# A bank of its own for p5 in the inner Strassen level of a float32 encoder block

## The chip, the core and the metric

The kernel runs on one core of one Trainium2 chip. The metric is the time of one execution on the device, in microseconds (us). The median of three runs of the kernel before is given below, and beside it one further execution that was recorded by the hardware profiler. Engines are named as in the profile: PE multiplies matrices, PEld loads its weights, ACT and DVE do elementwise work, SP issues transfers. A "bank" is a PSUM buffer of 128 partitions x 512 float32 numbers, into which PE adds its products.

## The reference

The reference is one layer of an encoder on 1024 tokens of width 1024, in float32: a SwiGLU pair around a token mixer, all with RMS norms and residual sums.

```python
h = x + 0.5 * swiglu_ffn(rmsnorm(x), ffn1_w_in, ffn1_w_out)      # hidden width 2816
proj = rmsnorm(h) @ w_in                                         # 1024 -> 7168: q k v g p and two gates
ret = retention(rotary(q), rotary(k) / 16, v)                    # 4 heads of 256, chunks of 64
ret = rmsnorm_per_head(ret) * silu(g)
pool_out = multiscale_pool(p, pool_w, pool_scale)
merged = sigmoid(gate_0 + b0) * (ret @ w_ret_up) + sigmoid(gate_1 + b1) * (pool_out @ w_pool_up)
h = h + merged @ w_out
h = h + 0.5 * swiglu_ffn(rmsnorm(h), ffn2_w_in, ffn2_w_out)
return rmsnorm(h)
```

Nearly all of the work is in the matrix products with the weights.

## The kernel before

**Products.** Activations lie with features on the 128 partitions and tokens along the row. Each float32 operand is split into a coarse part and a remainder (ACT casts, L151; DVE subtracts, L152), and one product of two such operands is three matmuls: coarse by coarse (L171), coarse by remainder (L172), remainder by coarse (L173), written together as `mm3`.

**The outer Strassen level.** The input products of both SwiGLU pairs and the combined projection are done by `strassen` (L391). One call, a group, makes two 128-row output tiles of 1024 tokens. It forms seven block products, each of 4 x 3 matmuls on 512 tokens, in place of eight. The banks of a group are `a`, `e` (from a pool of six, tag "ps") and the sum bank `b` (from a pool of two, tag "sum"). P3, the product of the weight combination S4 with the activation block R22, is the one on which the inner level works.

**The inner level.** `pairs` (L550) runs the groups two by two, first all steps of group A, then all of group B. For the pairs that share (`shared`), it leaves P3 out of both and runs `third` (L491) after them, which does P3 of A and B together with a second level of Strassen's scheme: seven products of half the width, 2 x 3 matmuls on 256 tokens each, so 42 matmuls. There are 8 such pairs in the first SwiGLU, 10 in the projection and 8 in the second SwiGLU, 26 in all; in this text each such call is "a third".

**Order within a third.** By the source, one third is these steps. `LO` and `HI` are the left and the right 256 columns of a 512-wide tile.

- p1: weights `wx`, six matmuls into the bank `x`, left half (L519). ACT copies that half to A's buffer `z` (L521).
- p5: weights `ws12` with the activation combination `y1`, six matmuls into the right half of the same bank `x` (L522). The first of them has no start flag. ACT copies this half to B's `z` (L524).
- p2: weights `wx`, six matmuls onto A's sum bank `b`, left half (L525).
- p6 (named so here): weights `ws12` with `y2`, six matmuls added to p1 in the left half of `x` (L529). DVE adds the copied p5 to it and writes A's `z`, right half (L531).
- Six matmuls with `ws34` onto A's `b`, right half (L532). Then DVE takes A's result out of `b` and `z` (L534, seen in the trace as line 631 or 990).
- Six matmuls with `wy` onto B's `b`, left half (L538).
- p7 (named so here): weights `ws34` with `y3`, six matmuls added to the left half of `x` (L539). ACT copies it to B's `z`, left half (L541), DVE adds to B's `z`, right half (L542), and B's result is taken out.

The weights of a third are split by `prep1` to `prep3`, which run four steps ahead of their products (`LOOK`, L51).

**What sets the order on an engine.** The source is written for a framework that orders each engine's queue and adds the waits between engines. An instruction can stand earlier in its queue than in the source when those before it are expected not to be ready; `soon()` (L98) raises the priority of what is inside it. In the trace of before, four of the six matmuls of p2 stand ahead of p5 on PE for this reason. Banks of a pool are handed out by the framework, and a bank is free again when the last reader of its holder is done.

**Names in the profile.** Buffer numbers are left out, so the bank `x` of a third is `a_x` in the first SwiGLU, `c_x` in the second, and `q0x`, `k0x`, `p1x` ... in the projection. The buffers `z` of both groups are `a_z` (or `c_z`) alike in the SwiGLUs; in the projection A's and B's have different names, as `q0z` and `t1z`.

Of the kernel before, what the change touches and what calls it, by code (L numbers as in the profile page):

```python
# [89 lines left out]
def block_kernel(ctx: ExitStack, tc, x, x_tok, vecs, f1_in, f1_out, w_in, pool_w, w_ret, w_pool, w_o,  # L90
# [6 lines left out]
    copy = nc.scalar.copy  # L97
# [25 lines left out]
    def c2(name):  # L123
        return sb.tile([P, H], F32, tag="c2", bufs=N_C2, name=name)

    def bank(name):
        return ps.tile([P, H], F32, tag="ps", name=name)

    def sum_bank(name):

        return ps.tile([P, H], F32, tag="sum", bufs=N_SUM, name=name)
# [10 lines left out]
    LO, HI = slice(0, HD), slice(HD, H)  # L142
# [20 lines left out]
    def weights(src, name):  # L163
        w = wt(name)
        n = src.shape[-1] // P
        split(flat(w, 0, n), flat(w, 1, n), src)
        return w

    def mm3(dst, w, m, start, stop):

        mm(dst, w[0], m[0], start=start, stop=False, skip_group_check=True)  # L171
        mm(dst, w[0], m[1], start=False, stop=False, skip_group_check=True)  # L172
        mm(dst, w[1], m[0], start=False, stop=stop, skip_group_check=True)  # L173

    def parts(m, at=slice(None)):
        return m[:, 0, at], m[:, 1, at]
# [12 lines left out]
    for n in range(N_SUM):  # L189
        b = sum_bank(f"set{n}")  # L190
# [300 lines left out]
    def third(nx, A, B):  # L491

        w, t, a, b = {}, {}, A.t, B.t

        def prep1():
            w["x"] = weights(a["S4"], f"{A.name}wx")
            s = t["s"] = c2(f"{A.name}s12")
            tt(s[:, LO], b["S4"][:, LO], b["S4"][:, HI], ADD)
            tt(s[:, HI], s[:, LO], a["S4"][:, LO], SUB)
            w["s12"] = weights(s, f"{A.name}ws12")  # L500

        def prep2():
            s = c2(f"{A.name}s34")
            tt(s[:, LO], a["S4"][:, LO], b["S4"][:, LO], SUB)
            tt(s[:, HI], a["S4"][:, HI], t["s"][:, HI], SUB)
            w["s34"] = weights(s, f"{A.name}ws34")

        def prep3():
            w["y"] = weights(b["S4"][:, HI], f"{A.name}wy")

        def prod(dst, n, at, m, start=False):
            for z in range(2):
                mm3(dst, parts(w[n], at + z), nx.block(m, z), start and z == 0, z == 1)


        def one():
            x = t["x"] = bank(f"{A.name}x")
            a["z"], b["z"] = c2(f"{A.name}z"), c2(f"{B.name}z")
            prod(x[:, LO], "x", 0, (0, 0), True)  # L519
            with soon():  # L520
                copy(a["z"][:, LO], x[:, LO])  # L521
            prod(x[:, HI], "s12", 0, "y1")  # L522
            with soon():
                copy(b["z"][:, HI], x[:, HI])  # L524
            prod(a["b"][:, LO], "x", 2, (1, 0))  # L525

        def two():
            x = t["x"]
            prod(x[:, LO], "s12", 2, "y2")  # L529
            with soon():  # L530
                tt(a["z"][:, HI], x[:, LO], b["z"][:, HI], ADD)  # L531
            prod(a["b"][:, HI], "s34", 2, (1, 1))  # L532
            with soon():
                A.third()  # L534

        def three():
            x = t["x"]
            prod(b["b"][:, LO], "y", 0, "y4")  # L538
            prod(x[:, LO], "s34", 0, "y3")  # L539
            with soon():  # L540
                copy(b["z"][:, LO], x[:, LO])  # L541
                tt(b["z"][:, HI], x[:, LO], b["z"][:, HI], ADD)  # L542
                B.third()

        return [(prep1, one), (prep2, two), (prep3, three)]


# [1079 lines left out]
```

## Time and profile before

| | |
|---|---|
| median of three runs | 2189.65 us (2189.18 to 2190.84) |
| profiled execution, its own time | 2191.3 us |
| its span on the core | 2189.3 us |
| DVE busy | 1788.2 us (82%) |
| ACT busy | 1038.8 us (47%) |
| PE clock granted, mean | 0.999 |
| transfers | 311.96 MB, 142 GB/s on the mean |

The profiled execution's own time is 2.0 us above its span. Every figure of an instruction below is from this execution. In a timeline the first column is the start in us from the span's beginning, the second the duration; in brackets stands how long the engine had been idle before the instruction, and who ended that. Matmuls overlap: a duration of 0.28 us goes with a start every 0.12 us, so a gap on PE is read from starts and not from the busy time.

### The profile page before, as it was taken

The page shows a single profiled execution, that of the slowest core. Times are in us where ns is not written, and L with a number is a line of the kernel's source. Part 1 is how long each engine was busy: PE and PEld are TensorE (multiplying, and loading weights), DVE is VectorE, ACT ScalarE, POOL GpSimd, SP SyncE. Part 2 cuts the span into 40 slices and gives each one's busy share as a digit, 9 for nine tenths or more (in the row PEclk, how much of TensorE's full clock was granted, in tenths as well). Part 3 has the DMA queues.
Part 4 walks back from the last instruction along what each step waited for, and adds up shares of the span by engine and source line. Part 5 has one row for each costly group of instructions (what it writes and reads, how often), then busy time and mean ns, then how long its engine had stood idle before and what let it go on. Part 6 is the DMA issues. An engine that isn't in the chain of part 4 may idle for free.

```text
span 2189.3 us, 29019 instructions
## 1 busy us (share of the span) xinstructions
PE 2176.3 (99%) x10556; PEld 1828.1 (84%) x10556; DVE 1788.2 (82%) x3068; ACT 1038.8 (47%) x1911; POOL 0.2 (0%) x4
## 2 busy tenths in 40 slices
PE   9999999999999999999999999999999999999998
PEld 7888888888888888888888998878888888888888
DVE  8797878888787687888887787799987878788774
ACT  8443434445554434344446663456633434344461
POOL 0000000000000000000000000000000000000000
PEclk9999999999999999999999999999999999999999
DMA  6233322596323332323345557524232322359522
GB/s 232 85 125 106 126 92 98 177 338 212 104 92 116 112 131 94 126 96 116 116 163 192 184 187 272 191 87 143 79 135 82 125 92 89 128 180 336 181 82 78
DMA packets 110447, 311.96 MB, mean 142 GB/s; under 512 B 12384, under 2 KB 13536, under 8 KB 110304
## 3 DMA queue, kind: packets, MB, share of 16 engines
q1 hardware_dynamic: 110304, 310.11, 41.4%
q8 instruction: 83, 1.36, 0.3%
q14 instruction: 60, 0.49, 0.1%
HBM read 219.36 MB, written 90.70 MB: 142 GB/s over the span
## 4 chain that ended last, share of the span: by engine, by line
PE 95%; DVE 2%; ACT 1%; DMA 1%; issue 0%; SPq 0%; DVEq 0%; ACTq 0%
PE c_b L171 2%; PE c_b L173 2%; PE c_b L172 2%; PE a_b L173 2%; PE a_b L172 2%; PE a_b L171 2%; PE c_a L172 2%; PE c_a L171 2%; PE c_a L173 2%; PE c_e L171 2%; PE c_e L172 2%; PE a_a L172 2%; PE a_a L171 2%; PE a_a L173 2%; PE a_e L173 2%; PE c_e L173 2%
## 5 line engine op out<-in xcount | busy, mean ns | idle before, releaser
L151 ACT CAST c_wS<-c_S 128x512 fp32r<-128x512 f32 x72 | 44.8, 622 | 70.8 <-DVE c_S L405 40.8
L172 PE MATMUL c_a<-n3R,c_wL 128*128 128x512 f32 x176 | 68.7, 390 | 0.0
L173 PE MATMUL c_a<-n3R,c_wL 128*128 128x512 f32 x176 | 68.5, 389 | 0.0
L172 PE MATMUL c_b<-n3T,c_wS 128*128 128x512 f32 x176 | 68.5, 389 | 0.0
L173 PE MATMUL c_b<-n3T,c_wS 128*128 128x512 f32 x176 | 68.5, 389 | 0.0
L171 PE MATMUL c_a<-n3R,c_wL 128*128 128x512 f32 x176 | 68.4, 390 | 0.0
L171 PE MATMUL c_b<-n3T,c_wS 128*128 128x512 f32 x176 | 68.2, 389 | 0.0
L171 PE MATMUL a_a<-n1R,a_wL 128*128 128x512 f32 x168 | 65.5, 390 | 0.0
L172 PE MATMUL a_a<-n1R,a_wL 128*128 128x512 f32 x168 | 65.5, 390 | 0.0
L171 PE MATMUL a_b<-n1T,a_wS 128*128 128x512 f32 x168 | 65.4, 389 | 0.0
L173 PE MATMUL a_b<-n1T,a_wS 128*128 128x512 f32 x168 | 65.4, 389 | 0.0
L173 PE MATMUL a_a<-n1R,a_wL 128*128 128x512 f32 x168 | 65.4, 389 | 0.0
L172 PE MATMUL a_b<-n1T,a_wS 128*128 128x512 f32 x168 | 65.4, 389 | 0.0
L151 ACT CAST a_wS<-a_S 128x512 fp32r<-128x512 f32 x68 | 42.1, 620 | 48.0 <-DVE a_S L405 24.2
L152 DVE TENSOR_TENSOR a_wS<-a_S,a_wS 128x512 fp32r<-128x512 f32 x68 | 46.3, 683 | 5.0 <-ACT a_wS L151 4.8
L152 DVE TENSOR_TENSOR c_wS<-c_S,c_wS 128x512 fp32r<-128x512 f32 x72 | 49.2, 684 | 1.2 <-ACT c_wS L151 1.0
L151 ACT CAST c_wL<-c_ra 128x512 fp32r<-128x512 f32 x44 | 27.1, 619 | 29.3 <-PE c_e L173 22.4
L151 ACT CAST a_wL<-a_ra 128x512 fp32r<-128x512 f32 x42 | 26.0, 621 | 29.8 <-PE a_e L173 22.6
L173 PEld LDWEIGHTS c_a<-n3R,c_wL 128*128 128x128 f32 x176 | 33.0, 188 | 6.9
L172 PEld LDWEIGHTS c_a<-n3R,c_wL 128*128 128x128 f32 x176 | 33.1, 188 | 6.9 <-DVE n3R L156 0.3
L172 PEld LDWEIGHTS c_b<-n3T,c_wS 128*128 128x128 f32 x176 | 33.0, 188 | 6.9
L171 PEld LDWEIGHTS c_b<-n3T,c_wS 128*128 128x128 f32 x176 | 33.0, 188 | 6.9
(2947 smaller groups left out, 7718.0 us busy)
## 6 DMA issues: line engine op xcount, KB each, us to landing
c_ra<-in_f_in SPq DMA_DIRECT2D x22, 512.0 KB, 3.6
c_rb<-in_f_in SPq DMA_DIRECT2D x22, 512.0 KB, 4.0
a_ra<-in_f_in SPq DMA_DIRECT2D x21, 512.0 KB, 3.9
a_rb<-in_f_in SPq DMA_DIRECT2D x21, 512.0 KB, 4.6
t<-au SPq DMA_DIRECT2D x11, 512.0 KB, 2.6
b<-an SPq DMA_DIRECT2D x11, 512.0 KB, 2.8
r<-au SPq DMA_DIRECT2D x11, 512.0 KB, 3.0
bra<-in_f_out SPq DMA_DIRECT2D x11, 512.0 KB, 5.9
```

What stands on the lines that cost most here:

```text
L151: copy(hi, src)
L152: tt(lo, src, hi.bitcast(F32), SUB)
L171: mm(dst, w[0], m[0], start=start, stop=False, skip_group_check=True)
L172: mm(dst, w[0], m[1], start=False, stop=False, skip_group_check=True)
L173: mm(dst, w[1], m[0], start=False, stop=stop, skip_group_check=True)
```

## The change

Within a third, p5 no longer goes to the right half of the bank `x`. A second bank `y` is taken from the pool of six at the same place, p5 goes to the right half of `y`, with a start flag of its own on its first matmul, and ACT's copy to B's `z` reads it there. The left half of `x` is used as before, its right half and the left half of `y` are not used. A pair with a third takes six banks from that pool in place of five. Nothing else is edited; the number of matmuls, copies, additions and transfers is the same.

```diff
         def one():
-            x = t["x"] = bank(f"{A.name}x")
+            x, y = (bank(f"{A.name}{n}") for n in "xy")
+            t["x"] = x
             a["z"], b["z"] = c2(f"{A.name}z"), c2(f"{B.name}z")
             prod(x[:, LO], "x", 0, (0, 0), True)
             with soon():
                 copy(a["z"][:, LO], x[:, LO])
-            prod(x[:, HI], "s12", 0, "y1")
+            prod(y[:, HI], "s12", 0, "y1", True)
             with soon():
-                copy(b["z"][:, HI], x[:, HI])
+                copy(b["z"][:, HI], y[:, HI])
             prod(a["b"][:, LO], "x", 2, (1, 0))
```

## The prediction

> **What bounds the kernel.** I read the page first, then the list of waits, then the timeline of one third. The page says that PE sets the time.
>
> ```profile
> span 2189.3 us, 29019 instructions
> ...
> PE 2176.3 (99%) x10556; PEld 1828.1 (84%) x10556; DVE 1788.2 (82%) x3068; ACT 1038.8 (47%) x1911; POOL 0.2 (0%) x4
> ...
> PE 95%; DVE 2%; ACT 1%; DMA 1%; issue 0%; SPq 0%; DVEq 0%; ACTq 0%
> ```
>
> The second line is busy time, the third the share of each engine in the chain that ended last. PE is on that chain for 95% of the span, so a gap removed from PE's queue shortens the time by its length, unless something else becomes late there. Such gaps are few, and the list of waits of PE's weight loads (us in total, times, longest) names most of them:
>
> ```profile
> PEld wo1b L171 <- ACT wo1wS L151: 2.1, 1, 2.1
> PEld c_x L171 <- ACT c_z L524: 2.0, 8, 0.2
> PEld a_x L171 <- ACT a_z L524: 1.9, 8, 0.2
> PEld a_x L171 <- ACT a_z L521: 1.6, 8, 0.2
> PEld c_x L171 <- ACT c_z L521: 1.5, 8, 0.2
> PEld xb L171 <- ACT state L151: 1.4, 2, 0.8
> ...
> PEld k0x L171 <- ACT t2z L524: 0.2, 1, 0.2
> ...
> PEld q1x L171 <- ACT q1z L521: 0.2, 1, 0.2
> ```
>
> Each third has two waits of the same kind: a product into `x` waits for ACT's copy out of `x` (L521 for the left half, L524 for the right). They come eight times each in both SwiGLUs, and the ten thirds of the projection have a row of 0.2 us each for L524 and for L521, of which one each is shown. Nothing else on PE repeats like this.
>
> The timeline of the first third shows what they cost:
>
> ```profile
> 139.72 0.28 PE L171 MATMUL a_x<-n1R,a_wx 128*128 128x256 f32 x1
> ...
> 140.32 0.28 PE L173 MATMUL a_x<-n1R,a_wx 128*128 128x256 f32 x1
> ...
> 140.69 0.37 ACT L521 COPY a_z<-a_x 128x256 f32<-128x256 f32 x1
> ...
> 140.80 0.28 PE L171 MATMUL a_b<-n1R,a_wx 128*128 128x256 f32 x1
> ...
> 141.12 0.19 PEld L171 LDWEIGHTS a_x<-n1y,a_ws 128*128 128x128 f32 x1 [0.24 <-ACT a_z L521]
> ...
> 141.34 0.28 PE L172 MATMUL a_x<-n1y,a_ws 128*128 128x256 f32 x1
> ...
> 142.30 0.28 PE L172 MATMUL a_b<-n1R,a_ws 128*128 128x256 f32 x1
> ...
> 142.56 0.19 PEld L171 LDWEIGHTS a_x<-n1y,a_ws 128*128 128x128 f32 x1 [0.19 <-ACT a_z L524]
> ...
> 142.78 0.28 PE L172 MATMUL a_x<-n1y,a_ws 128*128 128x256 f32 x1
> ...
> 143.26 0.28 PE L173 MATMUL a_x<-n1y,a_ws 128*128 128x256 f32 x1
> ...
> 143.65 0.42 DVE L531 TENSOR_TENSOR a_z<-a_x,a_z 128x256 f32<-128x256 f32 x1 [0.53 <-PE a_x L173]
> ...
> 145.30 0.40 PE L171 MATMUL a_a<-n1R,a_wL 128*128 128x512 f32 x1
> ```
>
> The six matmuls of p1 start from 139.72 to 140.32, and four matmuls of p2 follow, the last at 140.80. That is 1.08 us for nine steps, 0.12 us a step. p5 writes the right half, which the copy doesn't read, and yet its first weight load waits until the copy ends (140.69 + 0.37 = 141.06) and starts 0.06 us later. What is kept apart is thus the bank and not the columns. p6 then waits in the same way for the copy of p5, although it writes the left half.
>
> **Cost of the two waits.** From the matmul before the gap to the second one behind it, two steps at 0.12 us would be 0.24 us. The first gap takes 141.34 - 140.80 = 0.54, a loss of 0.30 us; the second 142.78 - 142.30 = 0.48, a loss of 0.24 us. About 0.2 us of each is the wait, and the rest is that the first matmul behind it needs 0.22 us to the next start. Together 0.54 us. The check is the third as a whole: 145.30 - 139.72 = 5.58 us for 42 matmuls, which at 0.12 us are 5.04 us, and 0.54 us remain. The last of the 26 thirds gives the same:
>
> ```profile
> 1921.89 0.28 PE L171 MATMUL c_x<-n3R,c_wx 128*128 128x256 f32 x1
> ...
> 1922.97 0.28 PE L171 MATMUL c_b<-n3R,c_wx 128*128 128x256 f32 x1
> ...
> 1923.46 0.28 PE L172 MATMUL c_x<-n3y,c_ws 128*128 128x256 f32 x1
> ...
> 1924.41 0.28 PE L172 MATMUL c_b<-n3R,c_ws 128*128 128x256 f32 x1
> ...
> 1924.95 0.28 PE L172 MATMUL c_x<-n3y,c_ws 128*128 128x256 f32 x1
> ```
>
> Here it is 0.49 - 0.24 = 0.25 and 0.54 - 0.24 = 0.30, 0.55 us. I take 0.545 us for each third.
>
> The step of 0.12 us is the row's. [...]
>
> **What goes, part by part.** p5 gets bank `y`, so it shares no bank with p1's copy, and the first wait goes. p6 adds to `x`; the copy of p5 now reads `y`, so the second wait goes as well. What p6 needs from then on is the copy of p1 (L521) alone. With no wait PE can follow the source: p1, p5, p2, p6 and so on. p6 would start 18 steps after 139.72, at 139.72 + 18 x 0.12 = 141.88, while that copy ends at 141.06: 0.76 us to spare after the 0.06 us of signalling.
>
> p5 would start six steps in, at 140.44 instead of 141.12. Its weights have long been there (first row):
>
> ```profile
> 133.58 0.68 DVE L152 TENSOR_TENSOR a_ws<-a_s,a_ws 128x512 fp32r<-128x512 f32 x1
> ...
> 139.95 0.68 DVE L631 TENSOR_TENSOR au<-a_e,a_v 128x512 f32<-128x512 f32 x1
> ...
> 142.44 0.68 DVE L637 TENSOR_TENSOR au<-au,n1rb 128x512 f32<-128x512 f32 x1
> ```
>
> Nothing is added on any engine: the same 42 matmuls, two copies, and the start flag is a field of a matmul that is there anyway. I cost the flag at nothing: p1's first matmul carries one and takes the same 0.28 us. No transfer moves.
>
> What is late next is p7, which adds to `x` and must wait for DVE's L531. p6's last matmul would start at 139.72 + 23 x 0.12 = 142.48. In before L531 starts 143.65 - 143.26 = 0.39 us after that start, so it would be ready at 142.87; the addition in front of it on DVE starts at 142.44 and such instructions start 0.6 us apart (757.21 and 757.82 below), so L531 runs from 143.04 to 143.46. p7 would start 36 steps in, at 144.04. That leaves 0.52 us after the signal. One third is tighter, the first of the projection, where a 1024-wide instruction stands ahead:
>
> ```profile
> 753.87 0.28 PE L171 MATMUL q0x<-n2R,q0wx 128*128 128x256 f32 x1
> ...
> 755.98 1.22 DVE L970 TENSOR_TENSOR cos<-cos,n2rb 128x1024 f32<-128x1024 f32 x1
> ...
> 757.21 0.69 DVE L152 TENSOR_TENSOR k0wS<-k0S,k0wS 128x512 fp32r<-128x512 f32 x1
> ...
> 757.82 0.42 DVE L531 TENSOR_TENSOR q0z<-q0x,t1z 128x256 f32<-128x256 f32 x1
> ```
>
> If DVE keeps that order, L531 ends at 758.24, and p7 would start at 753.87 + 36 x 0.12 = 758.19, so it waits about 0.1 us and loses 0.1 us at the restart: 0.2 us, once.
>
> The other engines must fit a shorter period. Two stretches of one pair with its third (PE, PEld, DVE, ACT busy, clock granted, DMA share):
>
> ```profile
> 139.72:177.96 38.24, 38.20 (x187) 32.17 (x186) 32.51 (x56) 15.35 (x27) 0.00 (x0) 1.00 0.37 138
> 1063.00:1101.20 38.20, 38.16 (x188) 32.13 (x187) 35.11 (x56) 17.31 (x38) 0.00 (x0) 1.00 0.31 111
> ```
>
> DVE's 32.51 us would lie in 37.7 us, and in the fuller one 35.11 in 37.65. DVE doesn't become the bound, and the clock was granted in full.
>
> **The sum.** 26 x 0.545 = 14.2 us, less 0.2 us for the one third: 14.0 us. The profiled execution would go from 2191.3 to 2177.3 us. It lies 1.65 us above the median of the runs, so the median would go from 2189.65 to 2175.65, which I give as 2175.7 us.
>
> **The rivals.** First, y's bank comes late. A pair would take all six banks of the pool where it took five. If y is given the bank that B's `e` has just left, p5 must wait for DVE's read of it (line 631 above, 139.95 to 140.63) and starts at 140.69 instead of 140.44: 0.25 us and 0.10 us for the restart, so 0.195 us of 0.545 are left, 5.1 us in all, 2184.6 us. For it speaks that the pool is now used to its full number; against it, that `e` of B and `x` are the only two of the six held then, and that both gaps of today end with a copy out of `x` and not with a reader of another bank. [...]
>
> Second, the change doesn't do what it says, and p5 and p6 wait for the copies as before, because the wait is tied to ACT's queue and not to the bank: 2189.7 us. Against it: the four matmuls of p2 run while the copy runs, so PE waits for no more than what touches `x`.
>
> Third, the other side: DVE's L531 takes the place of the waits. PE would reach it earlier, and what is queued on DVE may stand ahead of it. One more instruction of 0.60 us ahead uses up the 0.52 us that p7 has to spare. From 0.44 us of lateness on (0.545 less 0.10 for the restart) the change is a loss. Two instructions ahead make p7 late by 1.20 - 0.52 = 0.68 us and with the restart 0.78: 0.235 us more than today, 6.1 us over 26 thirds, 2195.8 us. For it speaks that DVE is busy 85% to 92% of these stretches and works in order; against it, that L531 was at the head of DVE's queue for 0.53 us before its input came, and that it is marked to go early.
>
> **How the numbers follow.** The forecast gets 0.85, the first rival 0.08, the second 0.04, the third 0.03. About 0.2% (4.4 us) is what a measurement of this kernel can tell from no change. The forecast and the first rival (5.1 us) are faster by more, so faster is 0.93, the same 0.04, slower 0.03. For the range, the two gaps read from starts rounded to 0.01 us give 0.52 to 0.57 us a third, 13.5 to 14.8 us. The order of other instructions may shift with the planning: the largest waits of PE outside the thirds, 2.1 us (`wo1b`) and 1.4 us (`xb`) in the list above, can grow or go. The lower end is 2189.65 - 14.8 - 2.1 = 2172.7 us (the larger one gone), the upper end 2189.65 - 13.5 + 0.2 + 3.5 = 2179.9 us (both doubled). It is the forecast's own range, and what it leaves out are the rivals, 0.15 together, and little of the forecast.
>
> **What would show it.** In the profile after, the list of waits has no rows of a product into `x` or `y` behind L521 or L524. On PE the six matmuls into `y` follow p1 at once and those of p2 come behind them. A third lasts 5.04 us and the thirds of a SwiGLU follow each other by 37.7 us, not 38.24. Rows of `y` behind line 631 would show the first rival, rows of `x` behind L531 the third. I am wrong if thirds shorten and the span does not: then something else on PE's path, a weight split or a transfer, would have been late all along.

## The result and the profile after

| | before | after |
|---|---|---|
| median of six runs each | 2190.32 us (2189.18 to 2191.17) | 2176.31 us (2175.06 to 2177.46) |
| profiled execution, its span | 2189.3 us | 2174.3 us |
| DVE busy | 1788.2 us | 1786.0 us |
| ACT busy | 1038.8 us | 1041.0 us |

The change makes the kernel faster. The medians differ by 14.0 us; the ratio is 0.9936 with a 95% interval of 0.9923 to 0.9949, which is 11 to 17 us. The kernel before has six runs now, so its median is 0.7 us above that of the first three.

The page of the kernel after, with the lines that answer to those shown of before:

```profile
span 2174.3 us, 29003 instructions
...
PE 2163.3 (99%) x10556; PEld 1825.3 (84%) x10556; DVE 1786.0 (82%) x3068; ACT 1041.0 (48%) x1911; POOL 0.2 (0%) x4
...
PE 96%; DVE 2%; ACT 1%; DMA 0%; issue 0%; SPq 0%; DVEq 0%; ACTq 0%
```

The counts of the five engines are the same. PE's share of busy time reads 99% in both, so this share doesn't show the gain at all; it has to be read from starts. The waits of PE's weight loads, of which the two that the prediction set against the thirds are shown:

```profile
PEld wo1b L171 <- ACT wo1wS L151: 2.1, 1, 2.1
PEld xb L171 <- ACT state L151: 1.3, 2, 0.8
```

These two are nearly as they were. All the rows of a product into `x` behind a copy are gone, in the SwiGLUs and in the projection, and no row of `y` is in the list. The line numbers of `third` are one higher now: the copies are L522 and L525, the addition L532. The timeline of the first third:

```profile
139.70 0.28 PE L171 MATMUL a_x<-n1R,a_wx 128*128 128x256 f32 x1
...
140.29 0.28 PE L173 MATMUL a_x<-n1R,a_wx 128*128 128x256 f32 x1
...
140.41 0.28 PE L171 MATMUL a_y<-n1y,a_ws 128*128 128x256 f32 x1
...
140.67 0.37 ACT L522 COPY a_z<-a_x 128x256 f32<-128x256 f32 x1
...
141.13 0.28 PE L171 MATMUL a_b<-n1R,a_wx 128*128 128x256 f32 x1
...
141.34 0.37 ACT L525 COPY a_z<-a_y 128x256 f32<-128x256 f32 x1 [0.29 <-PE a_y L173]
...
141.85 0.28 PE L171 MATMUL a_x<-n1y,a_ws 128*128 128x256 f32 x1
...
143.01 0.42 DVE L532 TENSOR_TENSOR a_z<-a_x,a_z 128x256 f32<-128x256 f32 x1
...
144.01 0.28 PE L171 MATMUL a_x<-n1y,a_ws 128*128 128x256 f32 x1
...
144.74 0.40 PE L171 MATMUL a_a<-n1R,a_wL 128*128 128x512 f32 x1
```

PE now follows the source: p1, p5, p2, p6. p5 runs in `y` from 140.41 on while ACT copies out of `x` at 140.67; before, it waited until 141.12. The third lasts 144.74 - 139.70 = 5.04 us in place of 5.58. The last third of the kernel says, beside the first, how the gain adds up:

```profile
1908.16 0.28 PE L171 MATMUL c_x<-n3R,c_wx 128*128 128x256 f32 x1
...
1913.19 0.40 PE L171 MATMUL c_a<-n3R,c_wL 128*128 128x512 f32 x1
```

The first third began 0.02 us earlier than in before (139.72), the last one began 1921.89 - 1908.16 = 13.73 us earlier, and it lasted 5.03 us in place of 5.58: 14.28 us by its end. The profiled spans differ by 15.0 us, 0.7 us more than that. One single wait of before, behind the last third, isn't there in after: a product `c_b` waits 0.83 us for DVE and starts at 1963.42 of the span of before.

```profile
PEld c_b L171 <- DVE cu L631: 0.8, 1, 0.8
```

The medians of six runs differ by 14.0 us and are too coarse to tell such a rest.

### The profile page after: what moved, and what is told of

Its sections match the earlier page's. It is cut to its first block, busy times and chain, and to the rows that moved or that the text cites. A ratio compares the mean times of both kernels' runs of the same rounds, so it can differ in the third digit from the quotient of the medians.

```text
span 2174.3 us, 29003 instructions
## 1 busy us (share of the span) xinstructions
PE 2163.3 (99%) x10556; PEld 1825.3 (84%) x10556; DVE 1786.0 (82%) x3068; ACT 1041.0 (48%) x1911; POOL 0.2 (0%) x4
## 4 chain that ended last, share of the span: by engine, by line
PE 96%; DVE 2%; ACT 1%; DMA 0%; issue 0%; SPq 0%; DVEq 0%; ACTq 0%
PE c_b L171 2%; PE c_b L173 2%; PE c_b L172 2%; PE a_b L172 2%; PE a_b L171 2%; PE a_b L173 2%; PE c_e L171 2%; PE c_a L172 2%; PE c_a L171 2%; PE c_a L173 2%; PE c_e L173 2%; PE c_e L172 2%; PE a_a L172 2%; PE a_a L171 2%; PE a_e L172 2%; PE a_e L171 2%
```

## The experiments

**The theory.** In a third, a product into the bank `x` waits on PE until ACT's copy out of `x` is done, though it writes other columns. From the last start of the product that is copied to the end of the copy and its signal it is 0.80 us (140.32 to 141.12 in before; at the other of the two places it is 0.74 us, 141.82 to 142.56); four matmuls in between cover 0.60 us of it. **The rivals**: the sixth bank matters as such; the two waits are one loss that moves from place to place; and the prediction's own, a late bank and a late addition. All times below are medians of five runs; before on the same chip, each time the median of nine runs, took 2189.67 us for the first four experiments and 2190.66 us for the last two.

**One bank, another order.** The edit is to the kernel before:

```diff
-            prod(x[:, HI], "s12", 0, "y1")
-            with soon():
-                copy(b["z"][:, HI], x[:, HI])
             prod(a["b"][:, LO], "x", 2, (1, 0))
+            prod(x[:, HI], "s12", 0, "y1")
+            with soon():
+                copy(b["z"][:, HI], x[:, HI])
...
+            prod(a["b"][:, HI], "s34", 2, (1, 1))
             prod(x[:, LO], "s12", 2, "y2")
             with soon():
                 tt(a["z"][:, HI], x[:, LO], b["z"][:, HI], ADD)
-            prod(a["b"][:, HI], "s34", 2, (1, 1))
```

> The kernel before with its bank x for both p1 and p5, but the products of a third in another order: p1, p2, p5, the one with ws34 and wy as they come, p6 behind the one with ws34. Six matmuls then stand on PE between p1 and p5 and six between p5 and p6 in place of four. Theory (a product into a bank waits for the end of the copy out of that bank, and four matmuls in between cover only 0.60 us of the 0.80 us that it takes): from the last start of p1 to p5 there are 7 x 0.12 = 0.84 us, the copy is done and signalled 0.80 us after that start, so both waits are gone without another bank: 14 us less than before, about 2176 us, thirds of 5.04 to 5.1 us. Rival (what counts is that there is one bank more to hold the sums): the waits stay, 2190 us.

Measured: 2178.85 us, 10.8 us below before, ratio 0.9952 (0.9940 to 0.9965). The second third of the first SwiGLU, around its two places:

```profile
177.67 0.28 PE L173 MATMUL a_x<-n1R,a_wx 128*128 128x256 f32 x1
...
177.99 0.37 ACT L521 COPY a_z<-a_x 128x256 f32<-128x256 f32 x1
...
178.39 0.28 PE L173 MATMUL a_b<-n1R,a_wx 128*128 128x256 f32 x1
178.51 0.29 PE L171 MATMUL a_x<-n1y,a_ws 128*128 128x256 f32 x1
...
179.82 0.28 PE L173 MATMUL a_b<-n1R,a_ws 128*128 128x256 f32 x1
179.94 0.30 PE L171 MATMUL a_x<-n1y,a_ws 128*128 128x256 f32 x1
```

p5 and p6 start 0.12 us behind the matmul ahead of them: with six matmuls in between there is no gap, in the very bank of before. So 10.8 us of the 13.5 us that the third experiment gains on the same chip come without another bank, and the rival falls that needs a sixth. Where the rest of 2.7 us lies, the list of waits and the end of the same third say:

```profile
PEld c_x L171 <- DVE c_z L532: 1.8, 8, 0.2
PEld a_x L171 <- DVE a_z L532: 1.6, 7, 0.2
```

```profile
181.34 0.42 DVE L532 TENSOR_TENSOR a_z<-a_x,a_z 128x256 f32<-128x256 f32 x1
...
181.86 0.34 PE L171 MATMUL a_x<-n1y,a_ws 128*128 128x256 f32 x1
182.04 0.28 PE L172 MATMUL a_x<-n1y,a_ws 128*128 128x256 f32 x1
```

p6 is later by six matmuls here, and with it DVE's addition, which p7 awaits. It ends at 181.76, just too late for p7, whose next step is 0.18 us in place of 0.12: a loss of 0.06 us, 1 us over the 16 thirds of the SwiGLUs (the first of them loses as much at p5 instead, where the copy ends a little later). It is the wait that the prediction's third rival named, at a small price. Most of the rest lies in the ten thirds of the projection. There the planner (the part of the framework that orders each engine's queue) put p6 behind the product with wy as well, and still it waits for the copy of p5, because ACT is busy with a longer instruction and starts that copy late. In the first of the ten:

```profile
751.87 1.15 ACT L1030 ACTIVATE t1B<-t1B,vec 128x1024 f32<-128x1024 f32 x1
...
752.93 0.35 ACT L525 COPY t1z<-q0x 128x256 f32<-128x256 f32 x1
...
753.33 0.19 PEld L171 LDWEIGHTS q0x<-n2y,q0ws 128*128 128x128 f32 x1
```

In four of the ten p7 also waits for DVE's addition. Counted over PE's starts (a step beyond the usual 0.12 us, or 0.23 us behind a matmul of 512 columns, is a loss), the ten thirds lose 2.5 us in this profile and the sixteen of the SwiGLUs 1.2 us, where the kernel after loses 0.2 us in each. So the 0.80 us hold only where ACT is free when the product is done; here it was 1.65 us, from p5's last start at 751.68 to 753.33.

**Only the first wait.** The first half of the edit above alone: p2 ahead of p5.

> The kernel before with p2 ahead of p5 in the source and nothing else moved: six matmuls stand between p1 and p5, four between p5 and p6 as before. Theory: the first wait goes and the second stays, so 0.25 to 0.30 us a third, 6.5 to 7.8 us, 2182.5 to 2183.8 us; the list of waits keeps the rows behind the copy of p5 and loses those behind the copy of p1. Rival (the waits are one loss that moves, so that curing one lengthens the other): 2190 us.

Measured: 2182.55 us, 7.1 us below before, ratio 0.9966 (0.9954 to 0.9979). The list of waits:

```profile
PEld c_x L171 <- ACT c_z L525: 1.6, 8, 0.2
PEld a_x L171 <- ACT a_z L525: 1.6, 8, 0.2
```

No row behind L521 is left, and the copy of p5 (L525 here) still holds p6 back eight times in each SwiGLU. In the second third PE's starts lose 180.46 - 179.97 = 0.49, less 0.24, 0.25 us at p6:

```profile
179.97 0.28 PE L171 MATMUL a_b<-n1R,a_ws 128*128 128x256 f32 x1
...
180.24 0.19 PEld L171 LDWEIGHTS a_x<-n1y,a_ws 128*128 128x128 f32 x1 [0.19 <-ACT a_z L525]
...
180.46 0.28 PE L172 MATMUL a_x<-n1y,a_ws 128*128 128x256 f32 x1
```

In the SwiGLUs the two waits are thus separate losses of about half each: by PE's starts the sixteen thirds lose 3.9 us in place of 8.8 us. The ten thirds of the projection don't test this. There the planner chose the order of the experiment before, with the late copies and additions shown there, and they lose 2.5 us in place of 5.5 us.

**Another bank, but no sixth.** The edit is to the kernel after; p5 goes to a bank that A has finished with long before.

```diff
-            x, y = (bank(f"{A.name}{n}") for n in "xy")
+            x, y = bank(f"{A.name}x"), a["e"]
```

> The kernel after, but p5 goes to the right half of the bank e of group A, which has been read long before, in place of a sixth bank. Theory (another bank than the one being copied is all that is needed): as after, 2176 us, no wait in the thirds. Rival (the sixth bank of the pool matters by itself): between 2176 and 2190 us, with waits on readers of e.

Measured: 2176.20 us, ratio to before 0.9940 (0.9927 to 0.9952), the time of after. The first third, from p1 to the next group:

```profile
139.34 0.28 PE L171 MATMUL a_x<-n1R,a_wx 128*128 128x256 f32 x1
...
140.05 0.28 PE L171 MATMUL a_e<-n1y,a_ws 128*128 128x256 f32 x1
...
144.37 0.40 PE L171 MATMUL a_a<-n1R,a_wL 128*128 128x512 f32 x1
```

It lasts 5.03 us. So no sixth bank is needed: one that nobody reads at that time did as well.

**A bank that is still being read.** The same with B's bank, which is the first rival of the prediction made on purpose.

```diff
-            x, y = (bank(f"{A.name}{n}") for n in "xy")
+            x, y = bank(f"{A.name}x"), b["e"]
```

> The kernel after, but p5 goes to the right half of the bank e of group B, which DVE is still reading when the third begins. This is the first rival of the prediction, made on purpose. As planned, two matmuls of p2 now stand ahead of p5, so that p5 could start 8 x 0.12 = 0.96 us after p1, and DVE's read ends and is signalled 0.97 us after p1's start. Theory: a wait of 0 to 0.1 us and up to 0.1 us for the restart, so 0 to 5 us above after, 2176 to 2181 us. The rival's own price, with nothing moved ahead: 0.35 us a third, 9 us above after, 2185 us.

Measured: 2178.86 us, 2.7 us above the experiment before this one, ratio to before 0.9952 (0.9939 to 0.9966). The first third:

```profile
140.27 0.68 DVE L632 TENSOR_TENSOR au<-a_e,a_v 128x512 f32<-128x512 f32 x1
...
140.87 0.28 PE L172 MATMUL a_b<-n1R,a_wx 128*128 128x256 f32 x1
...
141.07 0.19 PEld L171 LDWEIGHTS a_e<-n1y,a_ws 128*128 128x128 f32 x1
141.10 0.36 PE L171 MATMUL a_e<-n1y,a_ws 128*128 128x256 f32 x1
...
141.29 0.28 PE L172 MATMUL a_e<-n1y,a_ws 128*128 128x256 f32 x1
```

DVE's read ends at 140.95. p5 would have started at 140.99 and starts at 141.10, and its second matmul at 141.29 in place of 141.11: 0.18 us lost. The other 25 thirds lose 0.16 us each in this profile, 4.2 us in all; the medians show 2.7 us, and the profiled execution is the slowest of the five. The rival's wait is there, with about half the price that I gave it, since the planner moves two matmuls of p2 ahead.

**A late addition.** The edit is to the kernel after and makes the third rival on purpose. The addition is repeated; the output is the same.

```diff
-                tt(a["z"][:, HI], x[:, LO], b["z"][:, HI], ADD)
+                for _ in range(4):
+                    tt(a["z"][:, HI], x[:, LO], b["z"][:, HI], ADD)
```

> The kernel after, with DVE's addition behind p6 (line 531 of before) done four times in a row with the same result: 3 x 0.34 = 1.0 us more of DVE time ahead of p7 in each third. The third rival of the prediction, made on purpose. By the rival's sum (order on PE unchanged) p7 would be 1.0 - 0.52 = 0.5 us late and lose 0.1 us more at the restart: 0.6 us a third, 15 us above after, about 2191 us. My theory now: the planner moves matmuls of the next group ahead of p7 (eleven of 0.23 us as planned), p7 finds its input ready, and PE loses nothing: 2176 to 2178 us, thirds with the next group's matmuls among them and no wait behind that addition.

Measured: 2177.09 us, ratio to before 0.9940 (0.9927 to 0.9954), the time of after. The end of the first third:

```profile
144.59 0.28 PE L173 MATMUL a_b<-n1y,a_wy 128*128 128x256 f32 x1
...
144.72 0.40 PE L171 MATMUL a_a<-n1R,a_wL 128*128 128x512 f32 x1
...
146.51 0.41 DVE L533 TENSOR_TENSOR a_z<-a_x,a_z 128x256 f32<-128x256 f32 x1
...
147.01 0.39 PE L172 MATMUL a_a<-n1R,a_wL 128*128 128x512 f32 x1
147.24 0.28 PE L171 MATMUL a_x<-n1y,a_ws 128*128 128x256 f32 x1
```

The last of the four additions ends at 146.92, more than 2 us behind the place of p7 in the source. Eleven matmuls of the next group fill that time, p7 starts at 147.24 without a gap, and the three additions more, 0.41 or 0.42 us each in this third, cost nothing that the medians show. The forecast of no wait at all is missed by little: three thirds of the projection have a row of 0.2 us behind the addition (L533) in the list of waits, and by PE's starts all thirds together lose 0.4 us more than in the kernel after. So the order on PE isn't fixed when DVE gets later in the plan, and the price of 6 us in the prediction, worked out with a fixed order, was too high. What a lateness costs that the plan doesn't foresee isn't tested by this.

**Six banks wanted, five there.** The edit is to the kernel after.

```diff
-N_PS, N_SUM, N_IDLE = 6, 2, 6
+N_PS, N_SUM, N_IDLE = 5, 3, 6
```

> The kernel after, with five banks in the pool that a, e, x and y come from, and three sum banks in place of two. A pair with a third still takes six banks, now of five. Theory (at the third only e of B, x and y are held at once): the thirds stay at 5.03 us with no wait, 38.24 - 0.54 = 37.7 us from third to third, and the time is that of after, 2176 us, up to 4 us more where retention or the output products hold more banks at once. Rival (bank shortage): p5 or the next group's first product waits for a bank, at least 0.2 us a third, 5 us or more above after in the thirds alone.

Measured: 2177.83 us, ratio to before 0.9938 (0.9926 to 0.9951), not to be told from after. The first third:

```profile
139.66 0.28 PE L171 MATMUL a_x<-n1R,a_wx 128*128 128x256 f32 x1
...
140.38 0.28 PE L171 MATMUL a_y<-n1y,a_ws 128*128 128x256 f32 x1
...
144.70 0.40 PE L171 MATMUL a_a<-n1R,a_wL 128*128 128x512 f32 x1
```

It lasts 5.04 us. A pair takes six banks but doesn't hold six at once, so there is no shortage even with five.

## Why the prediction was right

- **The sum** was 14.0 us, and the medians differ by 14.0 us. That close a match of medians is luck, since their interval is 11 to 17 us. PE's starts are the sharper test: the 26 thirds last 145.0 us together in before and 130.9 us in after, so 14.0 us went where the prediction put them. Both waits went in all 26. The term of 0.545 us a third measures 5.58 - 5.04 = 0.54 us in the first and 5.58 - 5.03 = 0.55 us in the last.
- **The bank and not the columns**: the step that carried the forecast was read from the copy of the left half holding back a product into the right half. The order experiment and the two with other banks show both sides of it: the same bank cost nothing with six matmuls in between in the second third (a step of 0.12 us), and another bank cost nothing (5.03 us for the first third) unless it was being read too (0.18 us lost there). What the runs show is that this program's waits go by the bank. No run leaves such a wait out, so whether the chip itself needs it for columns that are apart isn't shown.
- **The new starts** were worked out by counting steps of 0.12 us. p5 was forecast at 140.44 and starts at 140.41, p6 at 141.88 and 141.85, DVE's addition at 143.04 and 143.01, p7 at 144.04 and 144.01; the whole third is 0.02 us earlier in this execution, which is most of the difference.
- **The one tight third**, the first of the projection, was mis-sized by half. I gave it 0.2 us by DVE's order of before. The planner moved the addition ahead of a weight split, and it ends at 753.35 + 0.42 = 753.77. p7 starts 0.01 us late, and only the restart is lost:

```profile
753.35 0.42 DVE L532 TENSOR_TENSOR q0z<-q0x,t1z 128x256 f32<-128x256 f32 x1
753.68 0.68 DVE L152 TENSOR_TENSOR k0wS<-k0S,k0wS 128x512 fp32r<-128x512 f32 x1
```

```profile
753.69 0.28 PE L173 MATMUL t1b<-n2y,q0wy 128*128 128x256 f32 x1
753.82 0.39 PE L171 MATMUL q0x<-n2y,q0ws 128*128 128x256 f32 x1
754.04 0.28 PE L172 MATMUL q0x<-n2y,q0ws 128*128 128x256 f32 x1
```

- **The rivals' prices** were too high, both for the same reason: they were worked out with PE's order held fixed. 0.35 us a third for a bank that is still read came out at 0.18 us in the first third and 0.16 us in the others, and a late addition at next to nothing.
- **What stays open** is the 0.7 us by which the profiled spans differ behind the last third. The single wait of 0.83 us there is about as large. It is also in the profile of the experiment that cured only the first wait, and in none of the others, so it seems to hang on the planned order; each of these is one execution, and no experiment isolates it.

## What to carry to other kernels

When a product and a copy share a bank, look at what runs between them on PE and not only at whether their columns are apart: here a product had to stand up to 0.80 us behind the last start of the one that is copied, so six matmuls of 256 columns in between, seven steps or 0.84 us, hid the copy and four, five steps or 0.60 us, didn't. That was so where ACT was free; in the first third of the projection it was busy for 1.15 us with another instruction, and twelve matmuls in between didn't hide the copy: p6 lost 753.55 - 753.11 - 0.24 = 0.20 us. Another bank that nobody read at that time removed the wait in every third (14.0 us by PE's starts), and enough independent matmuls in between removed most of it (10.8 us by the medians). Gaps of 0.24 to 0.30 us on an engine that was busy 99% by the page could be seen only in its starts, and they counted because they came 52 times.

## What the runs showed of the hardware

A short wait was nearly all restart here. In the tight third p7 was 0.01 us late, and the step to the matmul behind it took 754.04 - 753.82 = 0.22 us in place of 0.12. The weight loads of after show what goes with it. In the first row, where nothing waits, the load starts 0.11 us ahead of its matmul; in the second, that of p7, it starts with it:

```profile
753.58 0.19 PEld L173 LDWEIGHTS t1b<-n2y,q0wy 128*128 128x128 f32 x1
753.82 0.19 PEld L171 LDWEIGHTS q0x<-n2y,q0ws 128*128 128x128 f32 x1
```

The load for the matmul at 753.69 starts at 753.58, the load for the one at 753.82 only at 753.82. The addition that p7 awaits ended at 753.77, 0.04 us before p7 was due at 753.81, and still 0.10 us was lost on top of the wait of 0.01 us. In the two other cases shown above, the load is ahead by less than 0.11 us too: 141.07 for 141.10 behind DVE's read of B's bank, where the next step took 0.19 us, and in the second third of the order experiment 181.81 for 181.86, where it took 0.18 us:

```profile
181.81 0.19 PEld L171 LDWEIGHTS a_x<-n1y,a_ws 128*128 128x128 f32 x1 [0.23 <-DVE a_z L532]
181.86 0.34 PE L171 MATMUL a_x<-n1y,a_ws 128*128 128x256 f32 x1
```
